# A fused mixer and mixture-of-experts layer: mixer weights split by half chunks, experts gather from x, a ring of 19 pieces

## The chip, the cores and the metric

One Trainium2 chip; the program runs on one of its cores. The metric is the device time of one execution in microseconds (us), from the runs shown below. TensorE is called PE, VectorE DVE, ScalarE ACT, GpSimd POOL, and SyncE, whose queue issues the loads, SP. PEld is PE's loading of the stationary operand, which runs beside its matmuls.

## The reference, cut to what matters

```python
def reference(x, c, ...):                       # x: (1, 256, 1024) float32
    mod = (silu(c) @ w_mod + b_mod)             # six rows of 1024
    sh1, sc1, g1, sh2, sc2, g2 = split(mod, 6)
    h = rms_norm(x, norm_pre_mix) * (1 + sc1) + sh1
    proj = h @ w_in                             # 1024 x 5632: q, k, v, hg_q, hg_f, hg_i, hg_g, gate_a, gate_b
    ya = diff_attention(...)                    # 4 heads, block-causal, rotary
    yb = hgrn2(...)                             # gated linear recurrence, 4 heads
    y = (sigmoid(gate_a) * (ya @ w_branch_a) + sigmoid(gate_b) * (yb @ w_branch_b)) @ w_out
    x = x + g1 * rms_norm(y, norm_post_mix)
    h = rms_norm(x, norm_pre_ffn) * (1 + sc2) + sh2
    top_v, top_i = top_k(h @ router_w + router_b, 4)          # of 32 experts
    y = sum over a token's 4 experts e of  gate_e * (swiglu(h @ w_gate_up[e] + b_gate_up[e]) @ w_down[e] + b_down[e])
    return x + g2 * rms_norm(y, norm_post_ffn)
```

All 32 experts are run, each on the tokens that chose it. Everything is float32. One expert's `w_gate_up` (1024 x 2048) is 8 MB and its `w_down` (1024 x 1024) 4 MB, so the experts' weights are 384 pieces of 1 MB.

## The kernel before

**Memory.** Weights come into pieces of 128 partitions x 2048 float32 (1 MB). `NA = 16` pieces form an arena that lives as long as the kernel; during the mixer they hold weights that arrive, and also the mixer's own tensors. When the mixer is over, the pool `late` is closed and the pool `mo` opened in its place, and `mo` holds `NM = 2` further pieces. So the experts' weights go round a ring of 18 pieces. The list `slots` is that ring: `spot()` (called by `chunk`, L87) takes the next piece, and the DMA that SP issues for it (line L87 in every row) waits until the last reader of the piece's old content is done. `use(...)` sets the ring anew in the mixer; `slots.insert(...)` adds pieces as the mixer gives them up.

**The mixer's products** are made in a rounded float32 format, from two parts of each operand. For a chunk of weights of 128 x 2048, `split` (L116 to L123) writes `hi` by an ACT cast (L119) and `lo` by a DVE subtraction (L122); `split_between` does the same in two halves (L133, L134), with other work put before each half. `mm3` (L137) then issues three matmuls, hi by hi, hi by lo and lo by hi (L139 to L141). `hi` has three buffers of a whole chunk in `late`; `lo` lies in the arena pieces 11, 12 and 13. Of the mixer's weights, 27 chunks are split whole, and the others in halves. A projection (`proj`, L301) runs over the two half chunks of K (`kh`), in each over the two token tiles, and in each over four K tiles. The two branch products (L699 on) run token tile by token tile, branch b and then a in each; the first half of `w_out` (L802) likewise token tile by token tile.

**The end of the mixer.** x gets the mixer's result added (L763). `rstd` (L766) makes the factor of the second norm per token, r2, and ACT writes `xn2 = x * r2`, 128 x 1024 for each of the two token tiles (L833); `xn2` is a tile of its own. The router's logits give every token's place in the list of each expert (`posm`).

**Experts.** For each pair of experts `slot_is` (L894) writes one-hot rows: `oh[token, place] = (place == posm)`, one `tensor_tensor` of 128 x 192 (two experts of 96 places) for each token tile (L895). PE gathers the experts' tokens by matmuls of `xn2` by these rows (`gathered`, L916; for the first pair L1099), and the eviction applies the norm's weight, scale and shift (L907, L908). `gate_up` runs on PE for 64 places (L948) or 32 (L958), `down` at L975 (64) and L983 (32). `weights` (L987) makes the rows that put an expert's result back, with the token's gate.

**What sets the order.** `seq(engine, ...)` fixes the order of the calls that it wraps on an engine; the scheduler places the others. SP works through its DMAs strictly in order: one that waits for its piece holds up all that are behind it.

Of the kernel before, what the change touches and what calls it, by code (L numbers as in the profile page):

```python
# [22 lines left out]
P = 128  # L23
# [19 lines left out]
NM = 2  # L43
# [6 lines left out]
def kernel(ctx, tc, a, out):  # L50
# [61 lines left out]
    now = lambda engine, f: f()  # L112

    parts = deque((11, 12, 13))

    def split(v, n, m, order=False):  # L116

        hi = late.tile([P, 2048], F32R, name="hi", bufs=3).rearrange("p (a b) -> p a b", b=m)
        (seq if order else now)(A, lambda: nc.scalar.copy(hi, v))  # L119
        lo = piece(parts[0], F32R).rearrange("p (a b) -> p a b", b=m)  # L120
        parts.rotate(-1)
        (seq if order else now)(V, lambda: nc.vector.tensor_tensor(lo, v, hi.bitcast(F32), ALU.subtract))  # L122
        return hi, lo  # L123

    def split_between(v, m, before):

        hi = late.tile([P, 2048], F32R, name="hi", bufs=3).rearrange("p (a b) -> p a b", b=m)
        lo = piece(parts[0], F32R).rearrange("p (a b) -> p a b", b=m)
        parts.rotate(-1)
# [5 lines left out]
        return hi, lo  # L135
# [49 lines left out]
    xn2 = const.tile([P, NT, D], F32, name="xn2")  # L185
# [109 lines left out]
    def win_half(i, kh, order=False):  # L295
        return split(win_chunk(i, kh), 4, 512, order)
# [4 lines left out]
    def proj(w):  # L301
        pp = [bank(psa) for t in range(NT)]
        for kh, (wh, wl) in enumerate(w):
            for t in range(NT):
                ts = slice(t * P, (t + 1) * P)
                for k in range(4):
                    K = 4 * kh + k
                    mm3(pp[t], (hTh[:, K, ts], hTl[:, K, ts]), (wh[:, k], wl[:, k]), K == 0, K == KD - 1)
        return pp

    def proj_T(pp, kh, w, hs=range(H), ks=range(4)):
        wh, wl = w
# [38 lines left out]
    wf = split_between(win_chunk(4, 0), 512, lambda kp: normed_split(kp, f[kp]))  # L351
# [6 lines left out]
    use(8, 9, 6, 10, 3)  # L358
# [13 lines left out]
    wf = split_between(wf, 512, lambda i: normed_split(2 + i, f[i]))  # L372
    wq = split_between(win_chunk(3, 1), 512, lambda i: None)
# [325 lines left out]
    for n in range(2):  # L699
        ns = slice(512 * n, 512 * (n + 1))  # L700
        wb, wa = [split(chunk(rows(a[w], 0, 4)[:, :, ns], 4, 512), 4, 512) for w in ("w_branch_b", "w_branch_a")]
        for t in range(NT):
            ts = slice(t * P, (t + 1) * P)
            for (wh, wl), (yh, yl), sig in ((wb, yT[0], sigb), (wa, yT[1], siga)):
                pp = bank(psa)
                for h in range(H):
                    last = mm3(pp, (yh[:, h, ts], yl[:, h, ts]), (wh[:, h], wl[:, h]), h == 0, h == H - 1)
                nc.vector.tensor_tensor(sig[:, t, ns], pp, sig[:, t, ns], ALU.mult)
            nc.vector.tensor_tensor(siga[:, t, ns], siga[:, t, ns], sigb[:, t, ns], ALU.add)
# [5 lines left out]
    slots.insert(3, 6)  # L715

# [12 lines left out]
    def w_out_half(n):  # L729
        ns = slice(512 * n, 512 * (n + 1))  # L730
        wo = [split(chunk(rows(a["w_out"], 512 * kh, 4)[:, :, ns], 4, 512), 4, 512) for kh in range(2)]

        def times(t, ks):
            ts = slice(t * P, (t + 1) * P)
            for K in ks:
                wh, wl = wo[K // 4]
                last = mm3(py[t][n], (mTh[:, K, ts], mTl[:, K, ts]), (wh[:, K % 4], wl[:, K % 4]), K == 0, K == KD - 1)
# [28 lines left out]
    def rstd(ms):  # L766
        r = small.tile([P, 1], F32, name="rh_r")
# [51 lines left out]
    r20 = rstd(mx[:, 0])  # L819
# [10 lines left out]
    r21 = rstd(mx[:, 1])  # L830
# [30 lines left out]
    for i, t in enumerate((14, 15, 11, 12, 13, 7)):  # L861
        slots.insert(2 + i, t)
# [4 lines left out]
    for i in range(NM):  # L867
        slots.insert(8 + i, NA + i)
# [407 lines left out]
```

## Time and profile before

| | |
|---|---|
| median of 3 runs | 1236.87 us (1235.04 to 1237.81) |
| the profiled execution's own time | 1234.81 us |
| span of the profiled execution, first to last instruction | 1232.7 us |
| PE, DVE, ACT busy | 1003.6 us (81%), 422.8 us (34%), 225.4 us (18%) |
| moved by DMA | 465.70 MB, mean 378 GB/s |
| granted clock of PE, mean | 0.933 of full |
| mixer and router | up to about 275 us (the first expert's L948 starts at 275.34 us) |
| experts | 275 to 1220 us |
| stream of weights ends | 1218.48 us; the last output follows it |

A group of instructions is read by its line, engine, operation, what it writes and reads (out<-in), its shape and count, then the busy time in us and the mean ns of one; behind the second bar stands the idle time of the engine just before them, with what ended it. A queue (SPq) that waits has a row of its own. [...]

### The profile page before, as it was taken

The numbers are of one execution on the slowest core, as the hardware profiler recorded it, in microseconds if no ns is written. First come the engines' busy times: TensorE is split into PE (matmuls) and PEld (weight loads), VectorE is DVE, ScalarE is ACT, GpSimd is POOL, SyncE is SP. The second block draws the span as 40 slices with busy tenths as digits, with TensorE's granted clock in tenths as the row PEclk, the third lists the DMA queues.
The fourth block names the chain that finished last, engine by engine and source line by source line (L and its number), as shares of the span: only waits on it lengthen the run. The fifth ranks groups of instructions, "written<-read, shape, count | busy, mean of one in ns | idle before, by whom it ended". The sixth has DMA issues, their size and how long they took to land. (4 is left out here: it accounts for less than half of the span.)

```text
span 1232.7 us, 17243 instructions
## 1 busy us (share of the span) xinstructions
PE 1003.6 (81%) x6774; PEld 520.9 (42%) x6774; DVE 422.8 (34%) x784; ACT 225.4 (18%) x401; POOL 26.0 (2%) x36
## 2 busy tenths in 40 slices
PE   6999989998779998887789879769776667777855
PEld 3777777874334333333333334323232222233312
DVE  3597789642222222323222232312222212122212
ACT  3553565341111000110000010000010000010001
POOL 1020000010000000000000000000000000000000
PEclk9998989989899999998999999988999887889978
DMA  9966668699999999799999999999999999999994
GB/s 352 317 220 226 230 244 319 263 374 379 394 421 422 423 422 422 308 403 377 422 421 423 422 422 422 423 422 425 422 421 421 423 422 422 416 415 421 419 417 173
DMA packets 100191, 465.70 MB, mean 378 GB/s; under 512 B 9716, under 2 KB 9814, under 8 KB 67256
## 3 DMA queue, kind: packets, MB, share of 16 engines
q1 hardware_dynamic: 100024, 463.31, 93.1%
q8 instruction: 125, 2.05, 0.6%
q14 instruction: 42, 0.34, 0.1%
HBM read 462.23 MB, written 1.05 MB: 376 GB/s over the span
## 5 line engine op out<-in xcount | busy, mean ns | idle before, releaser
L958 PE MATMUL bank<-piece,xg 128*32 128x512 f32 x1472 | 206.6, 673 | 65.0 <-DMA piece<-in_w_gate_up_dram 51.2
L948 PE MATMUL bank<-piece,xg 128*64 128x512 f32 x768 | 171.0, 597 | 3.8 <-PEq L1158 3.0
L1010 DVE TENSOR_TENSOR acc<-acc,bank 128x512 f32<-128x512 f32 x136 | 84.3, 681 | 247.0 <-PE bank L1007 247.0
L926 DVE TENSOR_SCALAR bank<-bank 128x256 f32<-128x256 f32 (+1 forms) x35 | 18.3, 524 | 368.2 <-PE bank L958 254.6
L958 PEld LDWEIGHTS bank<-piece,xg 128*32 128x32 f32 x1472 | 44.4, 116 | 204.7 <-DMA piece<-in_w_gate_up_dram 112.0
L948 PEld LDWEIGHTS bank<-piece,xg 128*64 128x64 f32 x768 | 56.1, 138 | 112.0 <-issue 101.0
L983 PE MATMUL bank<-piece,actT 128*32 128x256 f32 x1472 | 99.5, 421 | 4.1 <-DMA piece<-in_w_down_dram 2.0
L927 ACT ACTIVATE s<-bank 128x256 f32<-128x256 f32 (+1 forms) x32 | 14.8, 463 | 476.5 <-DVE bank L926 476.5
L916 PEld LDWEIGHTS bank<-oh,xn 128*128 128x128 f32 x512 | 86.2, 200 | 30.6 <-issue 20.8
L916 PE MATMUL bank<-oh,xn 128*128 128x192 f32 (+1 forms) x512 | 95.4, 342 | 0.4 <-DVE xg L908 0.4
L975 PE MATMUL bank<-piece,actT 128*64 128x512 f32 x384 | 85.0, 595 | 0.9
L139 PE MATMUL bank<-hi,piece 128*128 128x512 f32 x208 | 82.5, 403 | 2.5 <-ACT hi L119 2.5
L140 PE MATMUL bank<-piece 128*128 128x512 f32 x208 | 82.6, 397 | 2.1 <-DVE piece L122 2.1
L141 PE MATMUL bank<-hi,piece 128*128 128x512 f32 x208 | 82.6, 397 | 0.0
L983 PEld LDWEIGHTS bank<-piece,actT 128*32 128x32 f32 x1472 | 49.8, 121 | 48.4 <-issue 16.7
L967 PE MATMUL bank<-ident,s 128*128 128x128 f32 x88 | 16.9, 298 | 62.8 <-issue 30.5
L122 DVE TENSOR_TENSOR piece<-piece,hi 128x2048 fp32r<-128x2048 f32 x27 | 62.7, 2324 | 14.3 <-ACT hi L119 14.3
L1007 PE MATMUL bank<-y,gt 32*128 32x256 f32 (+1 forms) x544 | 49.2, 396 | 21.3 <-ACT y L1026 21.3
L119 ACT CAST hi<-piece 128x2048 fp32r<-128x2048 f32 x27 | 51.2, 1900 | 18.9 <-PE bank L141 16.2
L1007 PEld LDWEIGHTS bank<-y,gt 32*128 32x128 f32 (+1 forms) x544 | 33.4, 185 | 44.5 <-ACT y L1026 42.4
L975 PEld LDWEIGHTS bank<-piece,actT 128*64 128x64 f32 x384 | 26.5, 137 | 51.7 <-issue 46.8
L1026 ACT COPY y<-bank 128x256 f32<-128x256 f32 (+1 forms) x35 | 15.6, 445 | 176.8 <-PE bank L983 95.0
(267 smaller groups left out, 884.9 us busy)
## 6 DMA issues: line engine op xcount, KB each, us to landing
piece<-in_w_gate_up_dram SPq DMA_DIRECT2D x256, 1024.0 KB, 19.7
piece<-in_w_down_dram SPq DMA_DIRECT2D x128, 1024.0 KB, 19.6
piece<-in_w_in_dram SPq DMA_DIRECT2D x22, 1024.0 KB, 6.3
piece<-in_w_mod_dram SPq DMA_DIRECT2D x16, 1024.0 KB, 6.4
piece<-in_w_mod_dram SPq DMA_DIRECT2D x16, 512.0 KB, 6.9
piece<-in_w_out_dram SPq DMA_DIRECT2D x4, 1024.0 KB
piece<-in_w_branch_b_dram SPq DMA_DIRECT2D x2, 1024.0 KB
piece<-in_w_branch_a_dram SPq DMA_DIRECT2D x2, 1024.0 KB
```

The lines of the kernel that those rows point to most:

```text
L119: (seq if order else now)(A, lambda: nc.scalar.copy(hi, v))
L122: (seq if order else now)(V, lambda: nc.vector.tensor_tensor(lo, v, hi.bitcast(F32), ALU.subtract))
L139: nc.tensor.matmul(out, ah, bh, start=start, stop=False, skip_group_check=True)
L140: nc.tensor.matmul(out, ah, bl, start=False, stop=False, skip_group_check=True)
L141: return nc.tensor.matmul(out, al, bh, start=False, stop=stop, skip_group_check=True)
L916: last = nc.tensor.matmul(ph[:, j], xn2[:, t, k * P : (k + 1) * P], oh[:, t, cs], start=t == 0, stop=t == NT - 1)
L948: nc.tensor.matmul(pp[r : r + C], xg[:, k, :C], wg[k][:, 0, 512 * q : 512 * (q + 1)], start=False, stop=k == KD - 1, skip_group_check=True)
L958: nc.tensor.matmul(halves(po[U * q : U * q + U]), xg[:, k, s0 : s0 + U], quarter(wg[k][:, 0], q), start=False, stop=k == KD - 1, skip_grou ...
L975: nc.tensor.matmul(py[C * n : C * n + C], at[:, j, C * half : C * half + C], wd[kk // 2][:, kk % 2, 512 * n : 512 * (n + 1)], start=kk == ...
L983: nc.tensor.matmul(py[U * c : U * c + U, 0:256], at[:, j, U * q : U * q + U], wd[kk // 2][:, kk % 2, 256 * c : 256 * (c + 1)], start=kk == ...
L1007: nc.tensor.matmul(pcs[c][:, t], gt[r : r + n, t * P : (t + 1) * P], y[r : r + n, w : w + 256], start=True, stop=True)
L1010: nc.vector.tensor_tensor(acc[:, :, cs], acc[:, :, cs], pcs[c], ALU.add)
```

## The change

`split` always works in halves. `hi` and `lo` of a half are tiles of 128 x 1024 in `late`, with four buffers each; a caller gets a list of K tiles, and `split_between` is gone. So the arena pieces 11, 12 and 13 no longer hold `lo`. Piece 11 holds `xn2`, which is now used in the mixer alone, 12 and 13 join the mixer's ring (seven pieces instead of five from `use(12, 13, 8, 9, 6, 10, 3)` on), and 11 joins the ring when the branch products are done. The 8 KB per partition that `xn2` had in the constant pool go to `mo`, which gets `NM = 3` pieces: the ring of the experts has 19.

The loops of `proj`, of the branch products and of the first half of `w_out` run over pairs of K tiles, and inside over the token tiles; of the branches, b is done for both token tiles and then a.

The scaling of x by r2 (L833) is gone. `rstd` writes r2 into a constant tile, `slot_is` multiplies the one-hot rows by it (one `tensor_scalar` of 128 x 96 for each expert and token tile, four for a pair instead of two), and PE gathers from `x`. The rest keeps its code; lines of the changed kernel are 9 or 10 lower in the mixer and 3 lower in the experts.

```diff
-NM = 2
+NM = 3
...
+    def split(v, before=None, order=False):
+
+        now = seq if order or before else lambda engine, f: f()
+        parts = [], []
         for i in range(2):
-            before(i)
+            if before:
+                before(i)
+            hi, lo = (late.tile([P, 2, 512], F32R, name=n, bufs=4) for n in ("hi", "lo"))
             h = slice(2 * i, 2 * i + 2)
-            seq(A, lambda: nc.scalar.copy(hi[:, h], v[:, h]))
-            seq(V, lambda: nc.vector.tensor_tensor(lo[:, h], v[:, h], hi[:, h].bitcast(F32), ALU.subtract))
-        return hi, lo
+            now(A, lambda: nc.scalar.copy(hi, v[:, h]))
+            now(V, lambda: nc.vector.tensor_tensor(lo, v[:, h], hi.bitcast(F32), ALU.subtract))
+            for part, t in zip(parts, (hi, lo)):
+                part.extend((t[:, 0], t[:, 1]))
+        return parts
...
-    xn2 = const.tile([P, NT, D], F32, name="xn2")
+    xn2 = part(11, 0, NT, D)
+    r2 = const.tile([P, NT], F32, name="r2")
...
-        for kh, (wh, wl) in enumerate(w):
+        for K in range(0, KD, 2):
+            wh, wl = w[K // 4]
             for t in range(NT):
                 ts = slice(t * P, (t + 1) * P)
-                for k in range(4):
-                    K = 4 * kh + k
-                    mm3(pp[t], (hTh[:, K, ts], hTl[:, K, ts]), (wh[:, k], wl[:, k]), K == 0, K == KD - 1)
+                for k in (K, K + 1):
+                    mm3(pp[t], (hTh[:, k, ts], hTl[:, k, ts]), (wh[k % 4], wl[k % 4]), k == 0, k == KD - 1)
...
-    use(8, 9, 6, 10, 3)
+    use(12, 13, 8, 9, 6, 10, 3)
...
+        for (wh, wl), (yh, yl), sig in ((wb, yT[0], sigb), (wa, yT[1], siga)):
+            pp = [bank(psa) for t in range(NT)]
+            for h0 in range(0, H, 2):
+                for t in range(NT):
+                    ts = slice(t * P, (t + 1) * P)
+                    for h in (h0, h0 + 1):
+                        last = mm3(pp[t], (yh[:, h, ts], yl[:, h, ts]), (wh[h], wl[h]), h == 0, h == H - 1)
...
     slots.insert(2, 1)
     slots.insert(3, 6)
+    slots.insert(4, 11)
...
-    for t, r2 in enumerate((r20, r21)):
-        seq(A, lambda: nc.scalar.activation(xn2[:, t], x[:, t], AF.Copy, scale=r2))
...
-    for i, t in enumerate((14, 15, 11, 12, 13, 7)):
+    for i, t in enumerate((14, 15, 7)):
         slots.insert(2 + i, t)
...
-        return nc.vector.tensor_tensor(oh, iota[:, None, s0 : s0 + n].to_broadcast([P, ne, n]),
-                                       posm[:, t, e0 : e0 + ne].unsqueeze(2).to_broadcast([P, ne, n]), ALU.is_equal)
+        for i in range(ne):
+            last = nc.vector.tensor_scalar(oh[:, i], iota[:, s0 : s0 + n], posm[:, t, e0 + i : e0 + i + 1], r2[:, t : t + 1], ALU.is_equal, ALU.mult)
+        return last
...
-                last = nc.tensor.matmul(ph[:, j], xn2[:, t, k * P : (k + 1) * P], oh[:, t, cs], start=t == 0, stop=t == NT - 1)
+                last = nc.tensor.matmul(ph[:, j], x[:, t, k * P : (k + 1) * P], oh[:, t, cs], start=t == 0, stop=t == NT - 1)
```

Two places show how the instructions move. The first is SP's queue where the mixer ends: the loads of the branches' and `w_out`'s chunks, and the first pieces of the experts (`w_gate_up` of experts 0 and 1, `w_down` of expert 0), up to the branch into expert 0's code. Before:

```order
L87 DMA piece<-in_w_branch_a_dram 128x4x512
L87 DMA piece<-in_w_out_dram 128x4x512 x2
L87 DMA piece<-in_w_gate_up_dram 128x2048 x2
L87 DMA piece<-in_w_down_dram 128x2x1024 x2
L87 DMA piece<-in_w_out_dram 128x4x512 x2
L87 DMA piece<-in_w_gate_up_dram 128x2048 x10
L1158 UNCONDITIONAL_BRANCH
L1164 UNCONDITIONAL_BRANCH
```

And with the change:

```order
L87 DMA piece<-in_w_branch_a_dram 128x4x512
L87 DMA piece<-in_w_out_dram 128x4x512 x2
L87 DMA piece<-in_w_gate_up_dram 128x2048
L87 DMA piece<-in_w_down_dram 128x2x1024 x3
L87 DMA piece<-in_w_out_dram 128x4x512
L87 DMA piece<-in_w_down_dram 128x2x1024
L87 DMA piece<-in_w_out_dram 128x4x512
L87 DMA piece<-in_w_gate_up_dram 128x2048 x10
L1155 UNCONDITIONAL_BRANCH
L1161 UNCONDITIONAL_BRANCH
```

Four expert pieces stand ahead of the second pair of `w_out` in both; with the change all four `w_down` pieces of expert 0 are among the first, and its last `w_gate_up` pieces are among the ten behind `w_out` and the four behind the branch.

The second place is DVE and ACT around the gates (`gate(7)`, `gate(8)`: the sigmoids of a projection, `xn_115<-bank` before and `piece<-bank` after), where PE waits in the trace of before. ACT before:

```order
L590 ACTIVATE piece,sm_1007<-bank,nm 128x256 x4
L634 ACT_TABLE_LOAD
L634 ACTIVATE xn_115<-bank 128x512
L612 ACTIVATE s_118<-bank 128x512
L634 ACTIVATE xn_115<-bank 128x512
L119 CAST hi<-piece 128x2048
L590 ACT_TABLE_LOAD
```

ACT with the change:

```order
L121 CAST hi<-piece 128x1024
L603 ACT_TABLE_LOAD
L603 ACTIVATE s_119<-bank 128x512
L581 ACT_TABLE_LOAD
L581 ACTIVATE piece,sm_1050<-bank,nm 128x256 x4
L625 ACT_TABLE_LOAD
L625 ACTIVATE piece<-bank 128x512 x2
L121 CAST hi<-piece 128x1024 x2
```

DVE with the change, in the same place (L122 is the low half, L395 the products that are added up for the modulation of the next stage):

```order
L395 SCALAR_TENSOR_TENSOR piece<-piece,csil 128x1024
L583 RECIPROCAL ri_1087<-sm_1050 128x8
L395 SCALAR_TENSOR_TENSOR piece<-piece,csil 128x1024
L585 TENSOR_TENSOR cf_1089<-sm_1050,ri_1087 128x4
L122 TENSOR_TENSOR lo<-piece,hi 128x1024
L586 TENSOR_SCALAR cf_1089<-cf_1089,nlam 128x4
L395 SCALAR_TENSOR_TENSOR piece<-piece,csil 128x1024
L589 SCALAR_TENSOR_TENSOR acc<-piece,cf_1089 128x256 x4
L427 TENSOR_TENSOR gw_118<-bank,cols 128x8
L122 TENSOR_TENSOR lo<-piece,hi 128x1024
```

Before, the cast of the whole chunk stood behind the sigmoids of the projection ahead; with the change the cast of its first half stands ahead of the exponentials (L581) and sigmoids, while the low halves lie between the products of L395.

## Rows read from the trace of the kernel before

**Rows 1.** The page: busy time per engine
```profile
PE 1003.6 (81%) x6774; PEld 520.9 (42%) x6774; DVE 422.8 (34%) x784; ACT 225.4 (18%) x401; POOL 26.0 (2%) x36
```

**Rows 2.** Waits of SP's queue, whole span: us, times, longest
```profile
SPq L87 <- PE bank L948: 88.3, 43, 15.2
SPq L87 <- PE bank L975: 81.9, 32, 14.2
```

**Rows 3.** Windows of the MoE stage: columns as in the first line
```profile
core 0: us, PE busy (x) PEld busy (x) DVE busy (x) ACT busy (x) POOL busy (x), PEclk, DMA share, GB/s
...
275.00:280.00 5.00, 5.00 (x26) 1.80 (x26) 0.98 (x4) 1.33 (x2) 0.00 (x0) 1.00 0.81 304
...
515.00:520.00 5.00, 3.66 (x20) 1.70 (x22) 2.15 (x4) 0.74 (x2) 0.00 (x0) 1.00 0.02 3
560.00:565.00 5.00, 3.89 (x24) 0.97 (x28) 0.15 (x1) 0.00 (x0) 0.00 (x0) 0.50 0.58 200
...
1100.00:1120.00 20.00, 15.59 (x159) 6.57 (x159) 4.20 (x10) 1.22 (x4) 0.00 (x0) 0.95 1.02 421
1200.00:1220.00 20.00, 16.78 (x132) 6.00 (x128) 2.13 (x6) 1.02 (x3) 0.00 (x0) 0.89 0.62 254
```

**Rows 4.** Waits of PE for pieces, 565 to 1220 us
```profile
PE bank L958 <- DMA piece<-in_w_gate_up_dram: 50.7, 47, 2.9
```

**Rows 5.** Timelines of SP, at 261 and 277 us
```profile
261.54 0.47 SPq L87 DMA_DIRECT2D piece<-in_w_gate_up_dram  x1
...
277.27 2.04 SPq L87 DMA_DIRECT2D piece<-in_w_gate_up_dram  x2
```

**Rows 6.** Timeline of PE, second half of expert 0
```profile
282.82 7.09 PE L948 MATMUL bank<-piece,xg 128*64 128x512 f32 x32 [0.43 <-PEq L1158]
```

**Rows 7.** Waits of PE's weight loads for pieces, 277 to 565 us
```profile
PEld bank L958 <- DMA piece<-in_w_gate_up_dram: 2.8, 3, 1.4
...
PEld bank L948 <- DMA piece<-in_w_gate_up_dram: 1.4, 3, 0.8
```

**Rows 8.** Lines by form: the splits on DVE, then on ACT
```profile
L122 DVE TENSOR_TENSOR piece<-piece,hi 128x2048 fp32r<-128x2048 f32 x27 | 62.7, 2324 | 14.3 <-ACT hi L119 14.3
...
L134 DVE TENSOR_TENSOR piece<-piece,hi 128x1024 fp32r<-128x1024 f32 x6 | 7.2, 1220 | 0.4 <-ACT hi L133 0.3
...
L119 ACT CAST hi<-piece 128x2048 fp32r<-128x2048 f32 x27 | 51.2, 1900 | 18.9 <-PE bank L141 16.2 <-DMA piece<-in_w_in_dram 2.6
...
L133 ACT CAST hi<-piece 128x1024 fp32r<-128x1024 f32 x6 | 6.1, 1042 | 0.0
```

**Rows 9.** Windows of the mixer
```profile
155.00:160.00 5.00, 1.87 (x7) 0.89 (x6) 5.00 (x10) 3.78 (x4) 0.00 (x0) 1.00 0.60 193
160.00:165.00 5.00, 4.12 (x18) 3.83 (x19) 3.77 (x8) 2.95 (x6) 0.00 (x0) 0.51 0.39 104
165.00:170.00 5.00, 5.00 (x17) 4.18 (x18) 4.19 (x9) 1.69 (x4) 0.00 (x0) 0.50 0.94 306
170.00:175.00 5.00, 5.00 (x34) 4.44 (x34) 2.70 (x4) 2.53 (x6) 0.00 (x0) 0.97 0.78 314
...
200.00:205.00 5.00, 5.00 (x23) 4.09 (x23) 4.96 (x7) 2.11 (x2) 0.00 (x0) 1.00 1.05 406
```

**Rows 10.** Waits of PE, 150 to 200 us
```profile
PE bank L139 <- ACT hi L119: 2.5, 1, 2.5
PE bank L140 <- DVE piece L122: 1.7, 1, 1.7
PE bank L413 <- DVE piece L404: 1.2, 1, 1.2
```

**Rows 11.** Lines by form: combine rows, one-hot rows, scaling
```profile
L987 DVE TENSOR_SCALAR gd<-iota,posm,gates 128x128 f32<-128x128 f32 x64 | 19.3, 343 | 14.5 <-DVEq L1158 14.5
L895 DVE TENSOR_TENSOR oh<-iota,posm 128x192 f32<-128x192 f32 x32 | 10.0, 353 | 2.8 <-PE bank L916 2.1
...
L833 ACT ACTIVATE xn<-x,rh_r 128x1024 f32<-128x1024 f32 x2 | 2.2, 1143 | 0.0
```

More of the change, by code (lines that the diff above doesn't have):

```diff
@@ L295, in win_half @@
     def win_half(i, kh, order=False):
-        return split(win_chunk(i, kh), 4, 512, order)
+        return split(win_chunk(i, kh), order=order)
     def win(i, order=False):
@@ L316, in proj_T @@
                 K = 4 * kh + k
-                last = mm3(pp[h // 2][:, h % 2], (wh[:, k, hs], wl[:, k, hs]), (hTh[:, K], hTl[:, K]), K == 0 and h % 2 == 0, K == KD - 1)
+                last = mm3(pp[h // 2][:, h % 2], (wh[k][:, hs], wl[k][:, hs]), (hTh[:, K], hTl[:, K]), K == 0 and h % 2 == 0, K == KD - 1)
         return last
@@ L350 @@
     use(8, 9, 10)
-    wf = split_between(win_chunk(4, 0), 512, lambda kp: normed_split(kp, f[kp]))
+    wf = split(win_chunk(4, 0), lambda kp: normed_split(kp, f[kp]))
     wq = win_half(3, 0)
@@ L371 @@
     f = [normed(kp, ph[kp - 2], e) for kp, e in ((2, A), (3, V))]
-    wf = split_between(wf, 512, lambda i: normed_split(2 + i, f[i]))
-    wq = split_between(win_chunk(3, 1), 512, lambda i: None)
+    wf = split(wf, lambda i: normed_split(2 + i, f[i]))
+    wq = split(win_chunk(3, 1), order=True)
     lamv = late.tile([P, 4, 64], F32, name="lamv")
@@ L700 @@
         ns = slice(512 * n, 512 * (n + 1))
-        wb, wa = [split(chunk(rows(a[w], 0, 4)[:, :, ns], 4, 512), 4, 512) for w in ("w_branch_b", "w_branch_a")]
-        for t in range(NT):
[L703 to L708, printed above, removed]
+        wb, wa = [split(chunk(rows(a[w], 0, 4)[:, :, ns], 4, 512)) for w in ("w_branch_b", "w_branch_a")]
+        for (wh, wl), (yh, yl), sig in ((wb, yT[0], sigb), (wa, yT[1], siga)):
[5 more added lines that the diff above has]
+                        last = mm3(pp[t], (yh[:, h, ts], yl[:, h, ts]), (wh[h], wl[h]), h == 0, h == H - 1)
+            for t in range(NT):
+                nc.vector.tensor_tensor(sig[:, t, ns], pp[t], sig[:, t, ns], ALU.mult)
+        for t in range(NT):
             nc.vector.tensor_tensor(siga[:, t, ns], siga[:, t, ns], sigb[:, t, ns], ALU.add)
@@ L730, in w_out_half @@
         ns = slice(512 * n, 512 * (n + 1))
-        wo = [split(chunk(rows(a["w_out"], 512 * kh, 4)[:, :, ns], 4, 512), 4, 512) for kh in range(2)]
+        wo = [split(chunk(rows(a["w_out"], 512 * kh, 4)[:, :, ns], 4, 512)) for kh in range(2)]
         def times(t, ks):
@@ L736, in times @@
                 wh, wl = wo[K // 4]
-                last = mm3(py[t][n], (mTh[:, K, ts], mTl[:, K, ts]), (wh[:, K % 4], wl[:, K % 4]), K == 0, K == KD - 1)
+                last = mm3(py[t][n], (mTh[:, K, ts], mTl[:, K, ts]), (wh[K % 4], wl[K % 4]), K == 0, K == KD - 1)
             return last
@@ L764, in residual, with rstd @@
         seq(A, lambda: square_mean(junk(), x[:, t, ns], mx[:, t, n : n + 1]))
-    def rstd(ms):
-        r = small.tile([P, 1], F32, name="rh_r")
+    def rstd(ms, r=None):
+        r = small.tile([P, 1], F32, name="rh_r") if r is None else r
         v = small.tile([P, 1], F32, name="rh_v")
@@ L802 @@
     times = w_out_half(0)
+    for K in range(0, KD, 2):
+        for t in range(NT):
+            times(t, (K, K + 1))
     for t in range(NT):
-        times(t, range(KD))
         square(t, 0)
@@ L818 @@
     seq(V, lambda: nc.vector.tensor_copy(hT2[0][:, 4:8], ph[1]))
-    r20 = rstd(mx[:, 0])
+    r20 = rstd(mx[:, 0], r2[:, 0:1])
     seq(T, lambda: times(1, range(6, KD)))
@@ L829 @@
     seq(A, lambda: nc.scalar.copy(hT2[1][:, 4:8], ph[1]))
-    r21 = rstd(mx[:, 1])
+    r21 = rstd(mx[:, 1], r2[:, 1:2])
     largest(0, pl0, r20)
-    for t, r2 in enumerate((r20, r21)):
-        seq(A, lambda: nc.scalar.activation(xn2[:, t], x[:, t], AF.Copy, scale=r2))
     pr0 = []
@@ L867 @@
     for i in range(NM):
-        slots.insert(8 + i, NA + i)
+        slots.insert(5 + i, NA + i)
     nc.gpsimd.memset(acc, 0.0)
@@ L1098 @@
         for k in range(KD):
-            seq(T, lambda: nc.tensor.matmul(ph[k // 2][:, k % 2], xn2[:, t, k * P : (k + 1) * P], oh[:, t, 0:CA], start=t == k % 2 == 0,
+            seq(T, lambda: nc.tensor.matmul(ph[k // 2][:, k % 2], x[:, t, k * P : (k + 1) * P], oh[:, t, 0:CA], start=t == k % 2 == 0,
                                             stop=t == NT - 1, skip_group_check=True))
```

13 lines of the change are left out of this document (removed).

## The prediction

> **What bounds the kernel now.** I read the page's busy times first: PE is busy 1003.6 us, 81% of the span, DVE 34% and ACT 18% [rows 1]. That is a mean over stages with different limits, so next come the waits of SP's queue. Its longest single waits are for PE to give up a piece: 15.2 us on the matmuls of L948 and 14.2 us on L975 [rows 2]. The reader is to see there that SP had a piece to load and no place for it: the ring was full. The windows tell when. The stream runs at about 421 GB/s when it runs freely (1100 to 1120 us). It falls to 304 GB/s at 275, to 3 at 515 and to 200 at 560 us; from then on no window up to 1200 us shows a hole until the stream ends in the window 1200 to 1220 [rows 3]. So there are three stages.
>
> 1. Mixer and router, up to 275 us: PE, with DVE close behind.
> 2. Experts from 275 to 565 us: PE with a full ring, and the stream waits for it.
> 3. From 565 us on the stream: PE now waits 50.7 us at L958 alone for pieces [rows 4].
>
> The end therefore is set by the last release of a piece on which the stream stood still (about 564.5 us, inside the window with 200 GB/s [rows 3]) plus the bytes that come after it at a steady rate. What counts is how early that release comes, and which piece it lets go.
>
> **The change part by part.**
>
> *The 19th piece.* With 18 pieces, load n waits until piece n-18 is used up; with 19, until piece n-19 is. At the last full-ring wait the same release thus starts the load that is one further on in the stream, and everything after it is one piece nearer to its end. A piece is 1.0486 MB (1024 KB); at 421 GB/s [rows 3] that is 2.49 us. This holds only if the ring is full by then, with 19 as with 18. The 18th piece was issued at 261.54 us and the next could only be issued at 277.27 [rows 5]: 15.7 us without a free piece. One more piece fills 2.5 of these, so the ring stays full. Term: **-2.5 us**.
>
> *The order of the first pieces.* In SP's queue expert 0's `w_down` now goes ahead of its last `w_gate_up` pieces. Seven pieces are issued only when `w_out` is done, near 260 us; at 2.49 us each, and with about one more in front, the last lands near 260 + 8 x 2.49 = 280 us. PE starts the second half of expert 0's K, where that piece is the last of four, at 282.82 us and takes 7.09 us [rows 6], so it needs the piece at about 288. Nothing; the cover is some 8 us.
>
> *Stage 2 gets a gift.* Between 277 and 565 us PE's weight loads wait 2.8 us for pieces at L958 and 1.4 at L948 [rows 7], 4.2 us in all, at places where the ring had run low. A stream that is one piece ahead after each full-ring wait covers a wait of up to 2.5 us, and the longest was 1.4. But weight loads run beside matmuls, and not all of the wait is PE's: bounds 0 and 4.2. I take the middle, **-2.0 us**; it reaches the end, since the release at 564.5 comes that much earlier.
>
> *Halves in place of whole splits.* DVE: 27 x (2 x 1220 - 2324) ns = 27 x 116 ns = +3.1 us; ACT: 27 x (2 x 1042 - 1900) ns = +5.0 us [rows 8]. [...] On the path lies only what falls where DVE is full. It is full in windows such as 155 to 160 and 200 to 205 us (5.00 and 4.96 of 5 us) [rows 9]; 16 of the 27 splits lie in such stretches (55 to 95 and 150 to 215 us). 16 x 0.116 = 1.9 us is the upper bound, 0 the lower, and I take **+0.9**. ACT is not full there and has slack; nothing.
>
> *Waits of PE on a split.* PE waited once 1.7 us for a low half (L140 on L122, near 197 us) and once 2.5 us for a high half (L139 on L119), followed by 1.2 us on DVE at L413 [rows 10]. With halves the first matmuls of a chunk need only half a subtraction, 1.1 us earlier, and in the new order that subtraction also stands earlier. The 1.7 goes: **-1.7**. The 2.5 I leave: the cast of gate(8)'s first half now stands ahead of the exponentials on ACT, but DVE's low half stands behind a row of L395 products, so PE is released by DVE at about the same time. What is late next is that low half.
>
> *Loops over pairs of K.* The first token tile's bank is finished 6 matmuls later (42 of 48 instead of 36). 23 matmuls take 5 us [rows 9], so 6 x 0.22 = 1.3 us later the eviction begins. Where the next work waits for that on DVE it costs 1.3, elsewhere nothing: **+0.7**. In the branch products the new order gives b's two banks to DVE while a still runs; nothing.
>
> *xn2, r2 and the one-hot rows.* Two ACT scalings of 1143 ns go [rows 11]. ACT idles there; nothing. Four `tensor_scalar` of 96 come for two `tensor_tensor` of 192 (353 ns each). The nearest row is the combine's `tensor_scalar` of 128 (343 ns) [rows 11]: at most 4 x 343 - 2 x 353 = +0.67 us for each of 16 pairs of experts, 11 us of DVE beside 423 busy. The cover is DVE's idle time while it waits for PE in the experts; without it, it would be 11. Only the first pair's stands just ahead of the first gather: bounds 0 and +0.7, I take 0, since counts and the last expert ranks are made there too.
>
> *Sum.* -2.5 - 2.0 + 0.9 - 1.7 + 0.7 = **-4.6 us**, made against the profiled execution, 1234.81 us, which lies 2.06 below the median 1236.87. Forecast: 1236.87 - 4.6 = **1232.3 us**, -0.37%. What a measurement can tell from no change is some 0.2%, 2.5 us: faster is below 1234.4, slower above 1239.3.
>
> **The rivals.**
>
> *A. The piece alone.* The waits of [rows 7] lie beside matmuls and the mixer's terms cancel: -2.5 us, 1234.4, on the border. For: most of PEld's waits end under running matmuls.
>
> *B. Slower: the mixer's splits fall behind.* The buffers now hold two chunks ahead of PE instead of three. Where DVE is full, PE catches up with it, idles, and its clock falls. [...] So one such place costs 3.7 us of waiting [rows 10] and about 5 of slow clock: 8.7 us, later for all that follows, and no stream idles enough to give it back: 1232.3 + 8.7 = **1241 us**. It decides from the first new idle of PE that is as long as that one. Against: PE's other waits on splits are short. [...]
>
> *C. The mixer gains.* The same place the other way: the earlier cast removes the wait at 155 to 160 and with it the slow clock: 1232.3 - 8.7 = 1223.6; with half of it 1228. For: on ACT the cast has moved ahead. Against: DVE is full there (5.00 of 5).
>
> *D. The piece does nothing.* The stream has its hole elsewhere, or the mixer's +1.9, +1.3 and +0.7 eat the gain: no change, about 1236.9. Against: the waits of [rows 2].
>
> **How the numbers follow.** Forecast 0.40, A 0.17, B 0.15, C 0.18, D 0.10. Faster: 0.37 of the forecast, half of A and C, 0.64. Same: the rest of both and D, 0.21. Slower: B, 0.15. The range takes in the forecast, A, D (0.67) and the nearer parts of C and B: 1226 to 1240.5. Below it lies a full C, above it a full B.
>
> **What would show it.** Right: the next piece after the ring is full is issued about one piece further on, the stream's last hole is still near 560 us, earlier by 2 to 4 us in what follows, the stream ends near 1214, L122 has some 60 instructions of 1220 ns, L948 starts within 2 us of 275.3, and no wait on L122 near 197. Wrong: a window of the mixer at clock 0.50 that was at 1.00 (B), the windows 160 to 170 at 1.00 (C), a first L948 off by over 4 us, or a stream that ends at the same 1218.5 us (D).

## The result and the profile after

| | before | after |
|---|---|---|
| median of 10 runs | 1236.99 us (1235.04 to 1240.1) | 1244.09 us (1240.8 to 1249.18) |
| ratio | | 1.006, 95% interval 1.0039 to 1.0081 |
| profiled execution | 1234.81 us | 1242.41 us |
| its span | 1232.7 us | 1240.4 us |

The change made the kernel slower by 0.6%, about 7 us; I had forecast 4.6 us faster and a range that ended at 1240.5. Read view by view, the trace at first looks like the forecast. The busy times differ little from [rows 1]; DVE has 8 us more:

```profile
PE 1009.2 (81%) x6774; PEld 520.6 (42%) x6774; DVE 430.8 (35%) x843; ACT 227.7 (18%) x426; POOL 26.6 (2%) x36
```

PE's timeline around the first expert (compare [rows 6]; the row of its first half before stands in the second fence):

```profile
271.75 7.04 PE L945 MATMUL bank<-piece,xg 128*64 128x512 f32 x32
279.23 7.09 PE L945 MATMUL bank<-piece,xg 128*64 128x512 f32 x32 [0.43 <-PEq L1155]
```

```profile
275.34 7.04 PE L948 MATMUL bank<-piece,xg 128*64 128x512 f32 x32
```

The first expert begins at 271.75 us, 3.6 us earlier than before. In the mixer PE waits less; the waits from 45 to 275 us, with changed lines (compare [rows 10]):

```profile
PE bank L130 <- DVE lo L122: 3.3, 2, 2.9
PE bank L466 <- POOL piece L463: 2.4, 4, 1.1
```

The wait near 197 us is gone. The other is still there, now on DVE's low half, and PE's clock falls after it as before: to 0.50 at 160 to 165 us, where it was 0.51 [rows 9]. The mixer's windows (columns as in [rows 9]; PEclk is the clock granted to PE as a share of its full clock):

```profile
155.00:160.00 5.00, 2.10 (x7) 1.47 (x7) 5.00 (x10) 3.68 (x5) 0.00 (x0) 0.76 0.27 79
160.00:165.00 5.00, 5.00 (x21) 4.52 (x22) 2.85 (x7) 1.55 (x4) 0.00 (x0) 0.50 0.86 287
165.00:170.00 5.00, 5.00 (x25) 4.15 (x24) 3.08 (x7) 1.40 (x6) 0.00 (x0) 0.72 0.55 187
195.00:200.00 5.00, 5.00 (x23) 4.04 (x22) 5.00 (x6) 3.47 (x4) 0.00 (x0) 1.00 1.04 396
```

The loss is further on. The windows of the experts (columns as in [rows 3]):

```profile
510.00:515.00 5.00, 2.48 (x25) 1.56 (x27) 2.91 (x5) 1.10 (x3) 0.00 (x0) 1.00 0.37 154
515.00:520.00 5.00, 5.00 (x26) 1.72 (x24) 0.00 (x0) 0.00 (x0) 0.00 (x0) 1.00 0.48 169
560.00:565.00 5.00, 4.97 (x32) 0.89 (x24) 0.00 (x0) 0.00 (x0) 0.00 (x0) 0.62 0.89 301
600.00:700.00 100.00, 84.03 (x514) 35.74 (x518) 25.41 (x54) 9.20 (x20) 0.00 (x0) 0.98 1.02 414
700.00:1200.00 500.00, 373.35 (x2898) 156.52 (x2890) 114.77 (x252) 43.92 (x106) 0.00 (x0) 0.88 1.01 412
1200.00:1220.00 20.00, 12.39 (x89) 3.91 (x90) 4.29 (x9) 0.76 (x2) 0.00 (x0) 0.83 0.89 358
```

And two windows of the kernel before that were not shown:

```profile
600.00:700.00 100.00, 83.80 (x511) 36.33 (x509) 25.29 (x52) 10.15 (x22) 0.00 (x0) 0.98 1.02 422
700.00:1200.00 500.00, 367.88 (x2930) 154.78 (x2934) 115.20 (x247) 44.29 (x107) 0.00 (x0) 0.90 1.02 421
```

The stream stands still around 510 to 520 us, as before, and dips once more at 560, to 301 GB/s where it fell to 200 [rows 3]. After that the stream, whose DMA engines are just as busy (share 1.02 and 1.01), moves 414 and 412 GB/s where it moved 422 and 421. From 600 to 1200 us that is 100 x 8 + 500 x 9 = 5300 GB/s x us, or 5.3 MB, less, and 5.3 MB at 412 GB/s take **12.9 us**. So the stream lost some 13 us, and the rest of the change must have gained some 6. In the window 1200 to 1220 us the stream, which had ended at 254 GB/s in the mean there, still runs at 358. It ends at 1226.62 us; before, it ended at 1218.48.

The DMA view of 700 to 1200 us shows the queue of the loads: packets, MB, and the time of the packets as a share of what 16 engines have. Before, and then with the change:

```profile
q1 hardware_dynamic: 37092, 209.26, 100.8%
```

```profile
q1 hardware_dynamic: 36393, 205.12, 100.6%
```

The engines are full in both, and with the change they finish fewer packets. Counted in the trace, a packet of 8192 bytes took 311.7 ns in the mean before and 317.1 ns with the change, in these 500 us. So it is the packet that takes longer.

What made the same loads 2% slower? No instruction of the experts' loads was changed. But the place where they land was. The arena follows the constant tiles in every partition. Before, it began at byte 48640, which is 95 x 512. The change takes the 8192 bytes of `xn2` out of the constants and puts in the tile `r2`, which is given 32 bytes: the arena begins at 40480, which is 79 x 512 + 32. So all 16 arena pieces lie 32 bytes off, and 8192 bytes of each piece are written in each partition. The three pieces in `mo` lie 480 over a multiple of 512, as the two did before.

### The profile page after: what moved, and what is told of

It reads as the page before. It is cut to its first block, busy times and chain, and to the rows that moved or that the text cites. A ratio compares the mean times of both kernels' runs of the same rounds, so it can differ in the third digit from the quotient of the medians.

```text
span 1240.4 us, 17345 instructions
## 1 busy us (share of the span) xinstructions
PE 1009.2 (81%) x6774; PEld 520.6 (42%) x6774; DVE 430.8 (35%) x843; ACT 227.7 (18%) x426; POOL 26.6 (2%) x36
## 2 busy tenths in 40 slices
DMA packets 100191, 465.70 MB, mean 375 GB/s; under 512 B 9716, under 2 KB 9814, under 8 KB 67256
## 5 line engine op out<-in xcount | busy, mean ns | idle before, releaser
L955 PE MATMUL bank<-piece,xg 128*32 128x512 f32 x1472 | 209.7, 684 | 66.7 <-DMA piece<-in_w_gate_up_dram 54.8
L913 PEld LDWEIGHTS bank<-oh,x 128*128 128x128 f32 x512 | 87.7, 203 | 31.7 <-issue 22.0
L913 PE MATMUL bank<-oh,x 128*128 128x192 f32 (+1 forms) x512 | 96.8, 346 | 0.4 <-DVE xg L905 0.4
L130 PE MATMUL bank<-lo,piece 128*128 128x512 f32 x208 | 84.1, 404 | 3.3 <-DVE lo L122 3.3
L122 DVE TENSOR_TENSOR lo<-piece,hi 128x1024 fp32r<-128x1024 f32 x60 | 74.0, 1254 | 16.7 <-ACT hi L121 16.5
L121 ACT CAST hi<-piece 128x1024 fp32r<-128x1024 f32 x60 | 62.0, 1047 | 45.0 <-PE bank L131 36.7
```

The source lines that it names most:

```text
L121: now(A, lambda: nc.scalar.copy(hi, v[:, h]))
L122: now(V, lambda: nc.vector.tensor_tensor(lo, v[:, h], hi.bitcast(F32), ALU.subtract))
L130: nc.tensor.matmul(out, ah, bl, start=False, stop=False, skip_group_check=True)
L913: last = nc.tensor.matmul(ph[:, j], x[:, t, k * P : (k + 1) * P], oh[:, t, cs], start=t == 0, stop=t == NT - 1)
L955: nc.tensor.matmul(halves(po[U * q : U * q + U]), xg[:, k, s0 : s0 + U], quarter(wg[k][:, 0], q), start=False, stop=k == KD - 1, skip_grou ...
```

## The experiments

### The arena's address

First theory: the start address of the pieces sets the stream's rate. The rival: the program does (a third piece in `mo`, the gather from x, the new order of the loads).

The changed kernel, with the arena back on a multiple of 512; every engine has the same instructions in the same order:

```diff
-    r2 = const.tile([P, NT], F32, name="r2")
+    r2 = const.tile([P, 128], F32, name="r2")
```

> The changed kernel with the same instructions on every engine; only the tile r2 takes 512 bytes of a partition instead of 32, so that the arena begins at byte 40960 (a multiple of 512) and no longer at 40480 (32 over a multiple of 512); before the change it began at 48640, a multiple of 512. Theory 1 (addresses): the stream ran at 413 to 415 GB/s after the change instead of 421 to 424 because the arena's pieces lie 32 bytes off; here it runs at 421 or more again and the time is about 1242.4 - 13 = 1229 to 1231 us, since all else of the change gained. Rival 2 (the program): a third piece in mo, the gather from x or the order of the loads slows the stream: it stays at 413 to 415 GB/s and the time at 1241 to 1245 us.

Measured: 1231.12 us (1227.73 to 1235.91, 12 runs) beside 1235.22 of before; ratio 0.9961 (0.9941 to 0.9982). The windows:

```profile
560.00:565.00 5.00, 4.75 (x32) 0.85 (x24) 0.00 (x0) 0.00 (x0) 0.00 (x0) 0.67 0.64 213
600.00:700.00 100.00, 84.35 (x522) 36.02 (x521) 25.31 (x53) 8.98 (x20) 0.00 (x0) 0.98 1.02 422
700.00:1200.00 500.00, 374.69 (x2942) 159.00 (x2931) 117.60 (x258) 44.30 (x107) 0.00 (x0) 0.89 1.02 420
1200.00:1220.00 20.00, 13.34 (x128) 5.66 (x124) 4.59 (x11) 4.36 (x17) 0.00 (x0) 0.97 0.39 159
```

The rate is back at 422 and 420, and the stream ends at 1213.66 us. 480 bytes of unused memory turn 0.6% slower into 0.4% faster.

The counterpart, the kernel before with one constant tile larger by 32 bytes:

```diff
-    gw2 = const.tile([P, KD], F32, name="gw2")
+    gw2 = const.tile([P, 2 * KD], F32, name="gw2")[:, 0:KD]
```

> The kernel before with the same instructions on every engine; only one constant tile is 32 bytes larger, so that the arena begins at byte 48672, 32 over a multiple of 512. Theory 1 (addresses): the stream falls from 421 to 424 GB/s to about 414, and with some 272 MB still to come after the last full ring the time rises by 272 MB x (1/414 - 1/422) = 12 to 13 us, to about 1249 us. Rival 2 (the program): the stream and the time stay, 1237 us.

Measured: 1253.02 us (1251.83 to 1254.57); ratio 1.0146 (1.0115 to 1.0177). The windows, and the start of the first expert:

```profile
600.00:700.00 100.00, 84.88 (x507) 37.23 (x502) 25.38 (x50) 11.19 (x24) 0.00 (x0) 0.98 1.02 414
700.00:1200.00 500.00, 371.79 (x2860) 152.06 (x2860) 114.79 (x245) 43.46 (x105) 0.00 (x0) 0.89 1.02 412
```

```profile
278.82 7.04 PE L948 MATMUL bank<-piece,xg 128*64 128x512 f32 x32
```

The kernel before, moved by 32 bytes, has the changed kernel's rate, 414 and 412. It lost 17.8 us in the profile's span, more than the 12 to 13 expected: its first expert begins 3.5 us later than that of before. Of the other 14.3 us, the two rates make 12.9 from 600 to 1200 us, as above. Of the 3.5, 2.0 are in PE's waits for the first `w_mod` pieces (L250, 3.6 us where they were 1.6). In the changed kernel the same offset did not move the first expert (271.75 us with it, 271.98 without), so that part is not settled. For the stream both directions agree, so the address is the cause and the program's other parts are not.

One rival remains in these edits: a wider constant tile also moves the constant tiles behind it, not only the arena. The largest of them is `acc`. It begins 32 bytes over a multiple of 512 in the kernel before, in the one with the arena at 40960 and in the counterpart, and their rates from 700 to 1200 us are 421, 420 and 412 GB/s; so `acc` does not set the rate. The smaller tiles between `acc` and the arena were not moved apart from it, but the packets of the run that moves `mo`'s pieces, further on, speak for the pieces.

How far off matters? The next kernels are the changed one with `r2` of other widths, so that the arena begins 64, 128, 256 and 480 bytes over a multiple of 512:

```diff
-    r2 = const.tile([P, NT], F32, name="r2")
+    r2 = const.tile([P, 16], F32, name="r2")
```

(16, 32, 64 and 120 elements for the four.)

> The changed kernel, same instructions; r2 takes 64 bytes, so that the arena begins at byte 40512, 64 over a multiple of 512. The arena at 32 over gave a stream of 412 to 414 GB/s and 1244 us, at 0 over 420 to 422 and 1231. Theory 1a (each piece's rows of 8192 bytes have to begin at a multiple of 64): 420 to 422 GB/s, 1231 us. Theory 1b (a multiple of 128, 256 or 512 is wanted): about 413 GB/s, 1243 us.

> The same with r2 of 128 bytes: arena at 40576, 128 over a multiple of 512. If 64 is enough or 128 is: 420 to 422 GB/s, 1231 us; if 256 or 512 is wanted: 413 GB/s, 1243 us.

> The same with r2 of 256 bytes: arena at 40704, 256 over a multiple of 512. If 256 or less is enough: 420 to 422 GB/s, 1231 us; only if 512 is wanted: 413 GB/s, 1243 us.

> The changed kernel, same instructions, with the arena at 40928, 480 over a multiple of 512, which is where the pieces of mo lie in both kernels. If every start that is no multiple of 256 costs the same: 413 GB/s and 1242 to 1246 us, and the three pieces in mo cost 3/16 of what the arena's offset costs, about 2 us. If 480 is harmless: 421 GB/s, 1231 us.

Each ratio is to runs of the kernel before that were made beside it:

| arena begins, bytes over a multiple of 512 | median us | ratio to before | interval |
|---|---|---|---|
| 0 | 1231.12 | 0.9961 | 0.9941 to 0.9982 |
| 32 (the change) | 1244.09 | 1.006 | 1.0039 to 1.0081 |
| 64 | 1242.38 | 1.0048 | 1.0033 to 1.0063 |
| 128 | 1245.83 | 1.0085 | 1.0071 to 1.01 |
| 256 | 1232.7 | 0.9962 | 0.994 to 0.9984 |
| 480 | 1244.93 | 1.009 | 1.0059 to 1.012 |

The window 700 to 1200 us of each, at 64:

```profile
700.00:1200.00 500.00, 370.18 (x2906) 155.71 (x2909) 114.96 (x254) 44.31 (x107) 0.00 (x0) 0.89 1.02 413
```

At 128:

```profile
700.00:1200.00 500.00, 367.91 (x2900) 155.97 (x2896) 116.47 (x257) 43.94 (x106) 0.00 (x0) 0.90 1.02 414
```

At 256:

```profile
700.00:1200.00 500.00, 365.08 (x2928) 151.58 (x2929) 117.97 (x261) 44.38 (x107) 0.00 (x0) 0.91 1.02 420
```

At 480:

```profile
700.00:1200.00 500.00, 376.01 (x2878) 157.61 (x2881) 114.69 (x252) 43.92 (x106) 0.00 (x0) 0.87 1.02 412
```

There are two groups and nothing between: 420 GB/s at 0 and 256, 412 to 414 at 32, 64, 128 and 480. The start 256 over is as good as the one at 0 (ratios 0.9962 and 0.9961), and the one 128 over is not (1.0085).

If 480 costs as much as 32, the pieces in `mo` cost their share too. The kernel with the arena at 40960 and `mo`'s pieces moved by 480 bytes:

```diff
-            w2 = mo.tile([P, D], F32, name="w2", bufs=1)
+            w2 = mo.tile([P, D + 120], F32, name="w2", bufs=1)[:, 0:D]
```

> As the run with the arena at 40960, and the three pieces in mo moved as well, from 480 over a multiple of 512 to a multiple of 512, by 480 bytes more in the tile w2 above them. Theory 1: 3 of 19 pieces were still off; if they cost as much each as the arena's, 2 per cent of 3/19 of the stream, the time falls by another 2 us against that run (stream 423 to 426 GB/s). If only the arena's offset of 32 matters and not one of 480, nothing changes. Rival 2: no change.

Measured: 1228.65 us (1226.45 to 1235.45, 12 runs); ratio 0.9955 (0.9936 to 0.9974). The median is 2.5 us lower, where 2 were expected, but the intervals of the two ratios lie almost on each other: the gain of these three pieces is not shown. Nor does the stream show it, whose rate was to rise to 423 to 426 GB/s and is nearly that of the run with only the arena moved (422 and 420):

```profile
600.00:700.00 100.00, 84.40 (x520) 35.78 (x516) 25.31 (x53) 8.89 (x19) 0.00 (x0) 0.97 1.02 423
700.00:1200.00 500.00, 371.37 (x2943) 156.09 (x2944) 117.68 (x258) 44.30 (x107) 0.00 (x0) 0.90 1.01 420
```

In the profile its first expert begins 1.5 us earlier (270.46 us), though `mo` is opened only after the mixer; so the mixer of a single profile varies by about that much, and part of the 2.5 us may be this.

The packets, counted in the traces, show that the expected share was too high. Of those of 8192 bytes from 700 to 1200 us, 11% took 309 ns or less in the changed kernel, 95% with the arena at 40960 and 98% with all pieces on multiples of 512. Had each packet into the three pieces in `mo` been slow, 3 of 19, or 16%, would have been. So these three pieces off the multiple among 16 on it cost far less each than when all are off (5% of the packets took more than 309 ns, beside 89% in the changed kernel); why is open. The slow packets do follow the pieces. With the arena at 40960, 77% of the packets that took more than 309 ns, from 600 to 1200 us, fall on five neighbouring pieces of every 19 of the stream; with the ring of 18 below, 70% fall on five of every 18. With all pieces on multiples of 512 no five of every 19 hold more than 48% of them.

It is the kernel with the lowest median of the study, and faster than both that it began with.

### The 19th piece

The changed kernel with the arena at 40960, and the one with all pieces on multiples of 512, each with a ring of 18:

```diff
-NM = 3
+NM = 2
```

> The changed kernel with the arena at 40960 and NM = 2: a ring of 18 pieces as before, all else as changed. It prices the 19th piece. My prediction's term was 2.5 us for the piece and 2.0 for the waits of PE that a stream ahead covers: 2.5 to 4.5 us slower than the run with 19 pieces and the arena at 40960. Rival (the piece is hidden): within 1 us of it.

> The run with all pieces on multiples of 512, with NM = 2: a second price of the 19th piece. The first pair gave 0.6 us between medians and 0.2 per cent, 2.6 us, between the ratios to before, while the ends of the streams in the two profiles lay 4.6 us apart. If the piece is worth one piece of stream, 2.5 us, this run lies at 1230.5 to 1232 us where 19 gave 1228.65; if it is worth the 2.0 of PE's waits as well, at 1233; if it is hidden, at 1228 to 1229.5.

Measured: 1231.72 us, ratio 0.9982 (0.996 to 1.0004), beside 0.9961 with 19 pieces; and 1231.26 us, ratio 0.9967 (0.9951 to 0.9982), beside 0.9955. By the ratios the piece is worth 0.21% and 0.12%, that is 2.6 and 1.5 us, each with an uncertainty larger than itself; between the medians lie 0.6 and 2.6 us. Both pairs have the sign of the term of 2.5 us, and it lies within what they allow, but neither alone proves it. In the profiles the stream of the run with 18 pieces still moves 248 GB/s in the mean from 1200 to 1220 us, where the one with 19 moved 159:

```profile
1200.00:1220.00 20.00, 16.33 (x140) 5.71 (x132) 2.61 (x7) 1.07 (x4) 0.00 (x0) 0.96 0.61 248
```

My second term, PE's waits that a ring of 19 would cover, found no support. The weight loads' waits for pieces from 275 to 565 us, with 19 pieces and the arena at 40960:

```profile
PEld bank L955 <- DMA piece<-in_w_gate_up_dram: 3.8, 6, 1.4
...
PEld bank L945 <- DMA piece<-in_w_down_dram: 2.2, 6, 0.8
...
PEld bank L945 <- DMA piece<-in_w_gate_up_dram: 1.8, 3, 1.2
```

and with 18, of which this is the longest row:

```profile
PEld bank L955 <- DMA piece<-in_w_gate_up_dram: 2.2, 2, 1.4
```

With 19 they are not shorter but longer, though PE begins the first expert at the same time in both (271.98 and 271.83 us). These are single profiles; the pair with all pieces on multiples of 512 shows the same. Why is open; no run was made for it.

### What brought the first expert forward

The changed kernel with the arena at 40960 begins its first expert at 271.98 us:

```profile
271.98 7.04 PE L945 MATMUL bank<-piece,xg 128*64 128x512 f32 x32
```

To see what brought that, I put back the loops of before in `proj`, the branch products and the first half of `w_out`, and kept the halves, the ring and the one-hot rows:

```diff
-        for K in range(0, KD, 2):
-            wh, wl = w[K // 4]
+        for kh, (wh, wl) in enumerate(w):
             for t in range(NT):
                 ts = slice(t * P, (t + 1) * P)
-                for k in (K, K + 1):
+                for k in range(4 * kh, 4 * kh + 4):
...
-    for K in range(0, KD, 2):
-        for t in range(NT):
-            times(t, (K, K + 1))
     for t in range(NT):
+        times(t, range(KD))
```

> The changed kernel with the arena at 40960, with the loops of before in the projections, the branch products and the first half of w_out (token tile outside, K tiles inside); the splits in halves, the ring and the one-hot rows stay as changed. Against the run with the arena at 40960 it prices the loops over pairs of K. That run's first expert began at 271.98 us, 3.4 us before the one of before. My prediction put the loops at +0.7 us, so without them the first expert would begin near 271.3 and the time be 0.7 us lower. Rival: the loops are what brought the 3.4 us, as each half of a chunk is used up after 12 matmuls instead of PE needing both halves before it turns to the other token tile: the first expert begins near 275 and the time is about 3 us higher, 1234.

Measured: 1236.33 us (1233.95 to 1240.97, 12 runs); ratio 1.001 (0.9993 to 1.0026). First expert and PE's waits from 45 to 275 us:

```profile
275.70 7.04 PE L939 MATMUL bank<-piece,xg 128*64 128x512 f32 x32
```

```profile
PE bank L465 <- POOL piece L462: 4.3, 3, 1.7
PE bank L403 <- DVE piece L394: 2.8, 1, 2.8
```

beside those with the new loops:

```profile
PE bank L130 <- DVE lo L122: 3.3, 2, 2.9
PE bank L466 <- POOL piece L463: 2.4, 4, 1.1
...
PE bank L404 <- DVE piece L395: 0.5, 1, 0.5
```

and, for POOL's work at the rope, with those of the kernel before:

```profile
PE bank L475 <- POOL piece L472: 2.5, 4, 1.3
```

The first expert begins 3.7 us later, at about the time of the kernel before (275.34), and the whole is 0.5% (0.9961 to 1.001) slower. So without the loops the rest of the change brings nothing at the first expert. PE waits longer at the rope (L465 for POOL, 4.3 against 2.4 us, and 2.5 in the kernel before) and at L403, 2.8 us for an L394 product, against 0.5 (1.2 before [rows 10]); in return the wait for the low half (L130) was 0.5 us there.

### The gather from x

The kernel with the arena at 40960 and 18 pieces, with the gather of before:

```diff
+    xg2 = mo.tile([P, NT, D], F32, name="xg2", bufs=1)
+    for t in range(NT):
+        seq(A, lambda: nc.scalar.activation(xg2[:, t], x[:, t], AF.Copy, scale=r2[:, t : t + 1]))
...
-        for i in range(ne):
-            last = nc.vector.tensor_scalar(oh[:, i], iota[:, s0 : s0 + n], posm[:, t, e0 + i : e0 + i + 1], r2[:, t : t + 1], ALU.is_equal, ALU.mult)
-        return last
+        return nc.vector.tensor_tensor(oh, iota[:, None, s0 : s0 + n].to_broadcast([P, ne, n]),
+                                       posm[:, t, e0 : e0 + ne].unsqueeze(2).to_broadcast([P, ne, n]), ALU.is_equal)
```

> The changed kernel with the arena at 40960 and 18 pieces, and the gather of before: ACT scales x by r2 into a tile of its own in mo (two instructions of 128 x 1024, ahead of the first pair's one-hot rows), the rows are one tensor_tensor of 128 x 192 for each token tile, and PE gathers from that tile. Against the run with 18 pieces and the arena at 40960 (1231.7 us) it prices the gather from x. My prediction put it at nothing, DVE's added time lying beside PE's work: within 1.5 us of that run, and DVE 6 to 12 us less busy. Rival: the four instructions in place of two stand on the path, in each pair of experts or ahead of the first gather: this run is 2 us or more faster.

Measured: 1231.81 us (1229.28 to 1238.24); ratio 0.9975 (0.9957 to 0.9992), beside 0.9982 with the gather from x: no difference. DVE was busy 423.9 us, where it was 430.3 with the gather from x. The one wait of PE that it adds in the mixer is that of the first gather for ACT's scaling, which stands later here than in the kernel before:

```profile
PE bank L1097 <- ACT xg L1087: 1.3, 1, 1.3
```

```profile
274.52 7.04 PE L943 MATMUL bank<-piece,xg 128*64 128x512 f32 x32
```

The second row is the first expert's start: 2.7 us later than the 271.83 of the run that it is compared with, and yet the time is the same. So a later first expert alone does not make the kernel slower by as much. That the 0.5% of the loops comes by way of their 3.7 us there is therefore not shown.

The changed kernel's rows cost, with its splits in halves:

```profile
L122 DVE TENSOR_TENSOR lo<-piece,hi 128x1024 fp32r<-128x1024 f32 x60 | 74.0, 1254 | 16.7 <-ACT hi L121 16.5
...
L892 DVE TENSOR_SCALAR oh<-iota,posm,r 128x96 f32<-128x96 f32 x64 | 18.1, 324 | 3.7 <-PE bank L913 2.0 <-DVE xg L905 0.8
```

That is 18.1 us of `oh` where it was 10.0 [rows 11]: 8.1 us more of DVE, hidden as I had put it. The splits took 74.0 us where they had taken 62.7 + 7.2 = 69.9 [rows 8]: 4.1 us more of DVE, where I had counted 3.1.

### A version that was to do better

PE's remaining wait for a split, 2.9 us at L130, lies behind products of L395 on DVE. With all pieces on multiples of 512, the calls of `aside`, which place these products, were moved behind `gate(8)`:

```diff
         nc.vector.tensor_tensor(sg[:, t], pg, sg[:, t], ALU.mult)
-    aside(2)
...
     gate(7, siga, 0)
-    aside(3)
...
     gate(8, siga, 1)
-    aside(1)
+    aside(6)
```

> All pieces on multiples of 512, and two of the calls that put the modulation's products (L395) beside the mixer moved from ahead of gate(8) to behind it, so that DVE reaches the low half of gate(8)'s first chunk two products (2 x 1.27 us) earlier. In the changed kernel PE waits there 2.9 us for that low half and its clock then stands at 0.50 for some 8 us. If the low half is what PE waits for, the wait falls under 1 us, the clock keeps 1.00 and the first expert begins 3 to 6 us earlier than 270.5; time 1223 to 1226 us. Rival: the products are only late elsewhere (the chunks they hold are released later, SP is held up, and PE waits for weights or for the modulation): 1228 to 1231 us or more.

Measured: 1234.83 us (1226.8 to 1238.64, 12 runs); ratio 0.9989 (0.9967 to 1.0011), beside 0.9955 for the same kernel without the move: 0.3%, or 4 us, slower, and 6 us between the medians. The rival came true. PE's waits from 45 to 275 us, the windows later in the mixer, and a wait of SP from 45 to 260 us:

```profile
PE bank L129 <- ACT hi L121: 3.9, 1, 3.9
PE bank L130 <- DVE lo L122: 2.8, 2, 2.4
```

```profile
185.00:190.00 5.00, 2.75 (x17) 2.11 (x15) 3.52 (x5) 3.69 (x7) 0.00 (x0) 1.00 0.01 2
190.00:195.00 5.00, 1.22 (x2) 0.50 (x2) 5.00 (x5) 5.00 (x6) 0.00 (x0) 0.52 0.60 170
195.00:200.00 5.00, 4.80 (x11) 3.80 (x12) 4.84 (x6) 0.47 (x2) 0.00 (x0) 0.50 0.87 305
```

```profile
SPq L87 <- DVE lo L122: 45.5, 12, 11.5
```

The wait has only gone elsewhere: at 190 to 195 us PE is busy 1.22 of 5 us, and its clock is 0.52 there and 0.50 in the next window. SP's waits for DVE's splits rise to 45.5 us (40.2 without the move), and at 185 to 190 us the loads stand still (2 GB/s). I read this as the products, now later, holding their chunks longer, so that those behind them in SP's queue come later too; that step was not tried by itself. The first expert begins at 277.27 us instead of 270.46.

## Why the prediction was wrong

**The step that failed** is the first one, which the whole sum stood on: that the end is the last release plus the bytes after it "at a steady rate". I took 421 GB/s from the rows and used it for the changed kernel without asking what sets it. The rate depends on where the pieces lie, and the change moves all 16 arena pieces by 8160 bytes, off their multiple of 512. In its place the runs showed: with the arena 32, 64, 128 or 480 bytes over a multiple of 512 the stream runs at 412 to 414 GB/s, and in the changed kernel, at 32, that costs 12.9 us from 600 to 1200 us alone. None of my rivals had it. Rival B gave a time of that order, 1241 us, by another mechanism, in the mixer, and that did not happen: the first expert began earlier. (The 5 us of slow clock in that sum are an estimate from [rows 9]: from 160 to 170 us, at 0.51 and 0.50, PE did 35 matmuls, and 34 in the next 5 us, at 0.97. In the changed kernel, at 0.50 and 0.72, it did 46 from 160 to 170 us.)

What a start off the multiple costs was measured in two ways: the rate is 2.0% lower from 700 to 1200 us (412 GB/s in the changed kernel, 420 with its arena at 40960), and a packet of 8192 bytes takes 1.7% longer there (317.1 ns in the changed kernel, 311.7 in the kernel before). A start 256 bytes over costs nothing (420 GB/s), one 128 over costs as much as one 32 over (414 and 412). What in the hardware makes it so was not tried here.

**With the rate put right**, the kernel with the arena at 40960 came out at 0.9961, which is -0.39%; the forecast was -0.37%. Its stream ended at 1213.66 us, where I had said near 1214. That the sum came so close is luck in part, since two of its terms were wrong and the first expert began 3.4 us earlier than in the kernel before, outside the 2 us that I had allowed:

- *The 19th piece*, -2.5 us: 2.6 and 1.5 us by the ratios of two pairs, 0.6 and 2.6 by their medians. Not contradicted, and too small to be resolved.
- *PE's waits that the ring covers*, -2.0 us: no run shows it. The weight loads waited longer with 19 pieces than with 18.
- *Halves in place of whole splits*, +0.9 us, and *the wait near 197 us*, -1.7: together -0.8. With the old loops the first expert begins at 275.70 us, 0.4 after the kernel before. The wait near 197 is gone, as forecast, while those at the rope and at L403 grew by 1.8 and 1.6 us; that what it gave came back there is argued from these rows. The wait near 158 us went from ACT's high half to DVE's low half, as forecast, 2.9 us where it was 2.5.
- *The loops over pairs of K*, +0.7 us: wrong in sign. They brought 3.7 us at the first expert and 0.5% in the end, though not shown to be the one by way of the other. Argued, not shown: I had counted the later end of the first bank, and not that each half is used up by both token tiles at once: its buffers come free sooner and the second half is needed later.
- *xn2, r2 and the one-hot rows*, 0: right for the time, though DVE got 8.1 us more.
- *The order of the first pieces*, 0: right; in the changed kernel's trace PE waits for no piece from 271 to 292 us.

## What to carry to other kernels

Before a steady rate is carried over to a changed kernel, write down what the change moves in memory: a small constant tile ahead of the buffers that a stream fills can cost more than the change gains. Here a tile of 32 bytes did (ratio 1.006, and 0.9961 with 480 bytes more): the stream ran at 420 to 422 GB/s with the arena 0 or 256 bytes over a multiple of 512, and at 412 to 414 with it 32, 64, 128 or 480 over. A pad of 224 or 480 bytes among the constants brought the rate back; streamed buffers placed first were not tried. And a loop that uses up a buffer for all its users at once was worth more here than the split that makes the buffer smaller: without the loops the first expert begins 3.7 us later and the ratio is 1.001 in place of 0.9961, while the rest of the change, the halves in it, leaves the first expert where it was (275.70 us, 275.34 before).

## What I had not expected of the hardware

The rate of loads into pieces with 8192 bytes in a partition fell from 420 to 422 GB/s to 412 to 414 when the arena's 16 pieces began 32, 64, 128 or 480 bytes over a multiple of 512, and not at 256. The packets and bytes of the whole execution (100191 and 465.70 MB) and the busy share of the DMA engines (1.02 and 1.01) do not show it. What does is the time of a single packet: 317.1 ns in the mean for 8192 bytes, where it was 311.7. And two or three pieces off the multiple among 16 on it cost the rate next to nothing: 420 or 421 GB/s from 700 to 1200 us with them (the kernel before and the one with the arena at 40960), 420 without.
